# A hybrid mLSTM/Hyena encoder block on one core: two-input elementwise work taken from GpSimd and given to VectorE

## The chip, the cores and the metric

The kernel runs on one core of a Trainium2 chip. The metric is the time of one execution on the device in microseconds (us). TensorE (PE) does the matrix products and transposes, VectorE (DVE) and ScalarE (ACT) the elementwise work, GpSimd (POOL) elementwise work, masks and some DMAs, and SyncE (SP) issues most of the DMAs. Each engine works through its own queue in order, and waits there for what the other engines deliver.

## The reference

One encoder layer on 512 tokens of width 1024, in fp32:

```
h  = rms_norm(x) * (1 + scale1) + shift1            # modulation from c @ w_ada
p  = h @ w_in + b_in                                # q, k, v, o, gates | x1, x2, z of Hyena
y_m = mLSTM(q, k, v, o, gates)                      # 4 heads x 128, forward + backward, chunkwise
z  = x1 * long_conv(z, filter0); z = x2 * long_conv(z, filter1); y_h = rms_norm(z)   # FFT convolution
x  = x + gate1 * (concat(y_m, y_h) @ w_out)
x  = x + gate2 * expert_choice_moe(rms_norm(x) * (1 + scale2) + shift2)   # 16 experts, 64 tokens each, ff 2048
out = rms_norm(x)
```

The weights of the 16 experts are 3 x 8 MB each and are read once.

## The kernel before

**Precision by halves.** In the projections an fp32 operand is split into a high half (fp32r, made by ScalarE's `act.copy` or a VectorE cast) and a low half, `lo = v - hi`. `split` (L240) does this for the weights: high half at L241 on ScalarE, low half at L242 on VectorE or GpSimd. A weight piece has 128 x 1024 elements. The same subtraction stands at L320 for the filter weights, at L499 for the tokens and at L848 for the mixer's result. The mLSTM result passes through `split` too (L804), always on VectorE.

**Front part.** Up to about 460 us the kernel computes filters and their spectra (`spectrum`, L359: sums and differences at L374/L376 from PSUM, combined by `put` at L383), the modulation (`ada`, L429; bias added at L452), the token operand (L491 to L500), the projections (`in_chunk`, L535, with the short convolution in `conv`, L560), the long convolutions (`long_conv`, L601: complex products at L615 to L617, `fold` and its `put` at L621), the heads (`stage`, `weighted`: scaling by the normaliser and sum of both directions at L786 to L795), Hyena's norm (L837), the output projection and the router.

**Order.** The phases are written in the order of `ORDER` (`Z C0 K Q X1 G I0 V C1 H0 H1 X2 I1 H2 O H3`). The Tile framework places the instructions in each engine's queue from a model of their times and from priorities; the output projection and the router are pinned by hand. Every instruction then runs in its queue's order.

**Two-input work on two engines.** The table `SHARE` (L113) has a pattern for each of eleven places, and `ew(site)` (L247) walks through it: a `p` puts the next instruction on GpSimd, a `v` on VectorE. What GpSimd does besides: masks (`affine_select`, L742 and L919), fills, the one-hot copies at L1233, one multiplication of 128 x 1024 per token tile (L984), and DMAs (L415, L450, L1110, L1121, L1145, L1167).

**Experts.** From about 460 us on, expert weights stream through a ring of eight 2 MB buffers (`ring`, L1079, SP's queue). A load into a buffer waits until TensorE has read what was there. The first loads also wait for space that the front part still holds.

Of the kernel before, what the change touches and what calls it, by code (L numbers as in the profile page):

```python
# [108 lines left out]
TEMPS = {"H": 4, "I": 3, "V": 2, "M": 5}  # L109

BANKS = {"P": 3, "S": 2, "R": 3}

SHARE = {"heads": "ppvvpppppvvvvvvv", "spectra": "vvvvvppp", "products": "vvpvpp", "folds": "vvpvvvvpvvppvvpv", "norm": "pppppvpv", "w3": "pvppvvpv", "filters": "p", "tokens": "vvpvvpvv", "w_in": "vp", "w_out": "vvpppppv", "mix": "vvvp"}  # L113

PACE = (1, 0, 2, 1, 1, 2, 1, 1, 1, 0, 2, 2, 2, 2)

# [17 lines left out]
def body(tc, a, out, dbg=None):  # L134
# [4 lines left out]
    with ExitStack() as ctx:  # L139
# [97 lines left out]
            k = i.shape[0]  # L237
            pin(pe.transpose(o, i, ident[0:k, 0:k]))  # L238

        def split(v, hi, lo, eng=None):  # L240
            act.copy(hi, v)  # L241
            (eng or dve).tensor_tensor(lo, v, hi.bitcast(F32), op=OP.subtract)  # L242


        _k = {}

        def ew(site):  # L247
            n = _k[site] = _k.get(site, -1) + 1
            return pool if SHARE[site][n % len(SHARE[site])] == "p" else dve

        def rstd_steps(o, v, ss, scale, eps, tag="rs"):

# [31 lines left out]
        with first(PF):  # L284
            hcol = hyp[:, H_B:H_B + 3]
            hid, sins = None, []
            for l in range(2):
                ps = bank("S")
                for q in range(2):
                    h = slice(64 * q, 64 * q + 64)  # L290
                    if l == 0:
                        mm(ps[h, 0:256], hyp[0:33, H_W1:H_W1 + 64], hyp[0:33, 256 * q:256 * q + 256])
                    else:
                        mm(ps[h, 0:256], hyp[h, H_W2:H_W2 + 64], hid[h, :])
                ar, kk = t2("H", n=256), t2("H", n=256)
                dve.tensor_scalar(ar, ps[:, 0:256], hcol[:, l:l + 1], hcol[:, 2:3], op0=OP.add, op1=OP.mult)
                dve.tensor_scalar(kk, ar, 1.0 / (2 * math.pi), MAGIC, op0=OP.mult, op1=OP.add)
                dve.tensor_scalar(kk, kk, MAGIC, None, op0=OP.subtract)
                c1 = 6.28125
                c2 = float(np.float32(math.floor((2 * math.pi - c1) * 2 ** 23) / 2 ** 23))  # L300
                c3 = 2 * math.pi - c1 - c2
                for c in (c1, c2, c3):
                    dve.scalar_tensor_tensor(ar, kk, -c, ar, op0=OP.mult, op1=OP.add)
                dve.tensor_scalar(ar, ar, 3.1415925, -3.1415925, op0=OP.min, op1=OP.max)
                hid = t2("H", n=256)
                sins.append(act.activation(hid, ar, AF.Sin).ins)


            hidp = t2("H", dt=F32R)
            his = [slice(64 * q, 64 * q + 64) for q in range(2)]  # L310
            for q, lo in enumerate(his[::-1]):
                hi, c = his[q], slice(256 * q, 256 * q + 256)
                dve.tensor_copy(hidp[hi, c], hid[hi, :])
                dve.tensor_tensor(hidp[lo, c], hid[hi, :], hidp[hi, c].bitcast(F32), op=OP.subtract)
            w3h, w3l = slot8("s", F32R), slot8("l", F32R)
            for b in (2, 3, 0, 1):
                bs = slice(b * 512, (b + 1) * 512)
                with tc.issue_after(sins[W3A]):
                    act.copy(w3h[:, bs], w3[:, bs])
                ew("w3").tensor_tensor(w3l[:, bs], w3[:, bs], w3h[:, bs].bitcast(F32), op=OP.subtract)  # L320

        sel4 = slot8("h", F32R)
        dve.tensor_copy(sel4[0:4, 0:512].rearrange("p (b m) -> p b m", b=4),
# [35 lines left out]
        def spectrum(Xc, Xs, uc, us, scale=None):  # L359

            def pair(u, cs, r, ops):

                p0, p2 = bank("S"), bank("S")
                mm(p2, dft(0, r + 2, cs), u[:, r + 2, :])
                mm(p0, dft(0, r, cs), u[:, r, :])
                f2 = t2("H")
                if scale is None:
                    act.copy(f2, p2)
                else:
                    act.mul(f2, p2, scale)  # L370
                o = [t2("H")] if len(ops) > 1 else []
                for v, op in zip(o + [f2], ops):
                    if scale is None:
                        dve.tensor_tensor(v, p0, f2, op=op)  # L374
                    else:
                        dve.scalar_tensor_tensor(v, p0, scale, f2, op0=OP.mult, op1=op)  # L376
                return o + [f2]

            both, add, sub = (OP.add, OP.subtract), (OP.add,), (OP.subtract,)

            def put(X, terms):
                for m, p, q, op in terms:
                    ew("spectra").tensor_tensor(X[:, m], p, q, op=op)  # L383

            ac, bc = pair(uc, 0, 0, both)
            cc, dc = pair(uc, 0, 1, both) if uc is us else pair(uc, 0, 1, add) + pair(us, 0, 1, sub)
            put(Xc, ((0, ac, cc, OP.add), (2, ac, cc, OP.subtract)))
            cs_, ds = pair(us, 1, 1, both) if uc is us else pair(us, 1, 1, add) + pair(uc, 1, 1, sub)
            put(Xc, ((1, bc, ds, OP.subtract), (3, bc, ds, OP.add)))
            as_, bs = pair(us, 1, 0, both)  # L390
            put(Xs, ((0, as_, cs_, OP.add), (2, as_, cs_, OP.subtract),
                     (1, bs, dc, OP.add), (3, bs, dc, OP.subtract)))

        KF = {}
        kfd = dp.tile([2, 128, 2048], F32, name="kfd")
        for o in (1, 0):
            plus, minus = q4(slot8("s")), q4(slot8("s"))
            for q in range(4):
                hs = []
                for d in range(2):  # L400
# [7 lines left out]
                        act.activation(wn, dab[:, bs], AF.Exp, scale=negt[:, q:q + 1])  # L408
                    dve.scalar_tensor_tensor(wn, wn, 0.05, ps, op0=OP.add, op1=OP.mult)
                    hs.append(wn)  # L410
                ew("filters").tensor_tensor(plus[:, q, :], hs[0], hs[1], op=OP.add)  # L411
                ew("filters").tensor_tensor(minus[:, q, :], hs[0], hs[1], op=OP.subtract)
                if q == 0:
                    hb = t2("I", 1, 512)
                    pool.dma_start(hb, a["hy_bias"][0, o:o + 1, :])  # L415
# [57 lines left out]
        with first(2000):  # L473
# [17 lines left out]
            for k in range(8):  # L491
                ps = bank("R")
                for i in range(4):
                    transpose(ps[:, i * 128:(i + 1) * 128], xt[i][:, k * 128:(k + 1) * 128])
                v = t2("I")
                act.activation(v, ps, AF.Identity, bias=mod1[:, 0, k:k + 1], scale=A1[:, k:k + 1])
                hi, lo = (t[k // 4][:, (k % 4) * 512:(k % 4 + 1) * 512] for t in (hh, hl))
                dve.tensor_copy(hi, v)
                ew("tokens").tensor_tensor(lo, v, hi.bitcast(F32), op=OP.subtract)  # L499
                hT.append((hi, lo))  # L500

        scr = dp.tile([2, 1024], F32, name="scr")
# [19 lines left out]
        def prep():  # L522

            if not halves:
                return
            c0, g = halves.pop(0)
            with first(PRIO):
                wh, wl = (slot8(t, F32R).rearrange("p (k c) -> p k c", k=8) for t in "hl")
                for t in (0, 4):
                    w = half2(n=4)  # L530
                    last_in[0] = sp.dma_start(w, w_in[:, t:t + 4, c0 + 256 * g:c0 + 256 * g + 256]).ins
                    split(w, wh[:, t:t + 4], wl[:, t:t + 4], ew("w_in"))
            ready.append((c0, wh, wl))

        def in_chunk(c0, done, tokens=False):  # L535
# [65 lines left out]
        def long_conv(u, o):  # L601
# [6 lines left out]
            for m in range(4):  # L608
# [3 lines left out]
                    act.dma_start(kf[:, m % 2], kfd[:, :, m * 512:(m + 1) * 512].rearrange("a p c -> p a c"))  # L612
                t = [t2("H") for _ in range(3)]
                for o_, p, q in ((t[0], c, kc), (t[1], s, ks), (t[2], c, ks), (s, s, kc)):
                    ew("products").tensor_tensor(o_, p, q, op=OP.mult)  # L615
                ew("products").tensor_tensor(c, t[0], t[1], op=OP.subtract)
                ew("products").tensor_tensor(s, t[2], s, op=OP.add)  # L617

            def put(terms):
                for o_, p, q, op in terms:  # L620
                    ew("folds").tensor_tensor(o_, p, q, op=op)  # L621

            def fold(Y):

# [146 lines left out]
        def weighted(h, d, pt):  # L771
# [11 lines left out]
            dve.reciprocal(nr, nr)  # L783
            nb = nr.unsqueeze(2).to_broadcast([128, 4, 128])
            if d == 0:
                ew("heads").tensor_tensor(hs4[:, :, h, :], pv[:, :, 0:128], nb, op=OP.mult)  # L786
                return
            ew("heads").tensor_tensor(pv[:, :, 0:128], pv[:, :, 0:128], nb, op=OP.mult)
            ew("heads").tensor_tensor(hs4[:, :, h, :], hs4[:, :, h, :], pv[:, :, 0:128], op=OP.add)
            for ti in range(4):  # L790
                junk = small(128, tag="jk", bufs=1)
                act.activation(junk, hs4[:, ti, h, :], AF.Square, accum_out=hss[:, ti, h:h + 1])
            hrs = small(4, tag="hrs")
            rstd(hrs, hss[:, :, h], 128, tag="r4")
            ew("heads").tensor_tensor(hs4[:, :, h, :], hs4[:, :, h, :], hrs.unsqueeze(2).to_broadcast([128, 4, 128]),  # L795
                              op=OP.mult)

        def head_out(h):
# [22 lines left out]
        def gated_2():  # L821
# [12 lines left out]
            zrs = small(16, tag="zrs", bufs=1)  # L834
            rstd(zrs, zss.rearrange("p r g -> p (r g)"), 128, tag="r16")
            for r in range(4):
                ew("norm").tensor_tensor(z2[:, r], z2[:, r], zrs[:, 4 * r:4 * r + 4].unsqueeze(2).to_broadcast([128, 4, 128]),  # L837
                                   op=OP.mult)
            mixh, mixl = slot8("s", F32R), slot8("s", F32R)
            for c in range(4):  # L840
# [4 lines left out]
                v = t2("H")  # L845
                act.activation(v.rearrange("p (i r) -> p r i", r=4), q4(ps), AF.Copy, scale=col(VG_H + c))
                dve.tensor_copy(mixT[4 + c][0], v)
                ew("mix").tensor_tensor(mixT[4 + c][1], v, mixT[4 + c][0].bitcast(F32), op=OP.subtract)  # L848

        def output_gates():  # L850
            def o_done(c, ps):
# [32 lines left out]
        for q, g, t0 in ((0, 1, "h"), (0, 0, "h"), (1, 1, "x"), (1, 0, "y")):  # L884
# [3 lines left out]
            for n in range(2):  # L888
                w = half2()
                sp.dma_start(w, w_out[:, 4 * g + 2 * n:4 * g + 2 * n + 2, q * 512:(q + 1) * 512])  # L890
                split(w, wh[:, 2 * n:2 * n + 2], wl[n], ew("w_out"))
            for k in range(4):
                wo[q, 4 * g + k] = (wh[:, k, :], wl[k // 2][:, k % 2, :])
        xt = load_x("aa")
# [387 lines left out]
```

## Time and profile before

| what | value |
|---|---|
| median of 3 runs | 1411.64 us (1408.95 to 1413.45) |
| profiled execution, its own time | 1409.65 us |
| its span (first to last instruction) | 1407.9 us |
| PE busy | 1292.6 us, 92% of the span |
| DVE busy | 530.3 us, 38%, 959 instructions |
| ACT busy | 255.7 us, 18% |
| POOL busy | 207.3 us, 15%, 174 instructions |
| HBM read | 460.53 MB, 330 GB/s over the span |

The busy shares are averages over a front part in which the elementwise engines work hard and an expert part in which they hardly work. Time in front of the span and behind it is 1409.65 - 1407.9 = 1.75 us. In the rows below, an instruction's duration is the time in the record of it; the next one on the engine often starts some 80 ns before the record ends.

### The profile page before, as it was taken

How to read it: one execution, taken by the hardware profiler on the slowest of the kernel's cores; microseconds unless marked ns; L12 is line 12 of the kernel's file. 1: busy time of each engine (PE TensorE's matmuls, PEld its weight loads, DVE VectorE, ACT ScalarE, POOL GpSimd, SP SyncE). 2: the span in 40 equal slices, each digit the busy share in tenths (PEclk: the TensorE clock that was granted, in tenths of full speed). 3: DMA queues.
4: the chain of work that ended last, by engine and by line, in shares of the span. 5: the costliest groups of instructions: out<-in, count | busy, mean ns of one | idle time of the engine just before them, and what ended most of it. 6: DMA issues, size and time to landing. Idle time of an engine off the chain costs nothing.

```text
span 1407.9 us, 14559 instructions
## 1 busy us (share of the span) xinstructions
PE 1292.6 (92%) x5845; PEld 602.2 (43%) x5845; DVE 530.3 (38%) x959; ACT 255.7 (18%) x557; POOL 207.3 (15%) x174
## 2 busy tenths in 40 slices
PE   6899989989695899999998999998999999899986
PEld 2366557657574333433432432343243343334322
DVE  6776895497837022212212122121122212212131
ACT  5333231336511010110100100001010010101110
POOL 5432671295502000000000000000000000000000
PEclk9999999999897999999999999999999999999999
DMA  9543444352515799999999999999999999999995
GB/s 329 184 172 120 155 140 122 128 187 77 198 61 209 311 399 427 426 428 427 426 427 427 427 426 426 426 426 429 425 427 426 427 427 427 427 426 426 427 410 223
DMA packets 57971, 466.07 MB, mean 331 GB/s; under 512 B 5416, under 2 KB 20008, under 8 KB 32432
## 3 DMA queue, kind: packets, MB, share of 16 engines
q1 hardware_dynamic: 53344, 455.56, 79.2%
q10 hardware_dynamic: 3216, 5.65, 1.3%
q0 software_dynamic: 1344, 3.94, 0.8%
q8 instruction: 46, 0.75, 0.2%
q14 instruction: 21, 0.17, 0.0%
HBM read 460.53 MB, written 4.60 MB: 330 GB/s over the span
## 4 chain that ended last, share of the span: by engine, by line
PE 60%; DMA 19%; DVE 11%; issue 5%; ACT 2%; POOL 2%; POOLq 0%; SPq 0%; ACTq 0%; DVEq 0%
PE ps L178 56%; DMA r<-in_w_up_dram 16%; PE ps L238 3%; DMA out_dram<-a 2%; DVE H L615 1%; DVE l L242 1%; DMA b<-in_hy_w_dram 1%; DMA M<-cmd 1%; DVE M L1228 0%; ACT I L1227 0%; DVE s L621 0%; POOL l L242 0%; DVE M L989 0%; DVE M L991 0%; POOL M L742 0%
## 5 line engine op out<-in xcount | busy, mean ns | idle before, releaser
L178 PE MATMUL ps<-r,x 128*64 128x512 f32 x2048 | 505.8, 611 | 37.8 <-DMA r<-in_w_up_dram 33.6
L178 PEld LDWEIGHTS ps<-r,x 128*64 128x64 f32 x2048 | 143.4, 139 | 306.1 <-issue 245.0
L178 PE MATMUL ps<-r,M 128*64 128x512 f32 x1024 | 231.9, 598 | 7.3 <-DVE M L1228 6.8
L1177 DVE SCALAR_TENSOR_TENSOR a<-ps,aff,a 128x512 f32<-128x512 f32 x120 | 90.1, 751 | 153.4 <-PE ps L178 153.4
L1233 POOL COPY H<-M 128x256 f32<-128x256 f32 x30 | 11.1, 400 | 807.5 <-DVE M L1187 606.6
L178 PEld LDWEIGHTS ps<-r,M 128*64 128x64 f32 x1024 | 69.1, 136 | 130.1 <-issue 117.5
L1217 DVE COPY I<-ps 128x512 f32<-128x512 f32 x32 | 22.1, 692 | 250.8 <-PE ps L178 231.8
L1219 ACT COPY I<-ps 128x512 f32<-128x512 f32 x32 | 18.8, 586 | 496.4 <-PE ps L178 496.4
L178 PE MATMUL ps<-b,h 128*128 128x512 f32 x192 | 83.8, 436 | 0.7 <-DVE b L499 0.6
L178 PE MATMUL ps<-a,h 128*128 128x512 f32 x192 | 81.7, 430 | 2.1 <-DVE x L566 2.1
L178 PE MATMUL ps<-a,l 128*128 128x512 f32 (+1 forms) x200 | 81.9, 410 | 0.0
L1228 DVE TENSOR_TENSOR M<-ps,I 128x256 f32<-128x256 f32 x64 | 27.2, 425 | 144.0 <-ACT I L1227 142.2
L178 PEld LDWEIGHTS ps<-M,h 128*128 128x128 f32 x512 | 63.3, 198 | 24.3 <-issue 18.6
L178 PE MATMUL ps<-M,h 128*128 128x128 f32 x512 | 68.9, 289 | 1.5 <-DVE M L1187 1.5
L178 PEld LDWEIGHTS ps<-V,H 128*128 128x128 f32 x120 | 22.3, 186 | 97.4 <-DVE a L1177 78.7
L178 PE MATMUL ps<-V,H 128*128 128x512 f32 x120 | 60.0, 500 | 0.0
L178 PE MATMUL ps<-s,d 128*128 128x512 f32 x112 | 57.5, 611 | 1.8 <-POOL s L411 1.1
L238 PEld LDWEIGHTS ps<-par,I 128*128 128x128 f32 x268 | 36.2, 208 | 47.9 <-issue 38.9
L1227 ACT ACTIVATE I<-ps 128x256 f32<-128x256 f32 x64 | 24.6, 384 | 167.4 <-PE ps L238 167.4
L238 PE MATMUL ps<-par,I 128*128 128x128 f32 x268 | 46.2, 305 | 7.5 <-DVE I L452 6.7
L242 POOL TENSOR_TENSOR l<-w,h 128x1024 fp32r<-128x1024 f32 x16 | 42.3, 2644 | 66.6 <-ACT h L241 51.1
L1102 DVE TENSOR_SCALAR x<-ps,A,mod 128x128 f32<-128x128 f32 x32 | 13.1, 410 | 99.5 <-PE ps L178 99.5
(329 smaller groups left out, 1369.6 us busy)
## 6 DMA issues: line engine op xcount, KB each, us to landing
r<-in_w_gate_dram SPq DMA_DIRECT2D x64, 2048.0 KB, 27.4
r<-in_w_up_dram SPq DMA_DIRECT2D x64, 2048.0 KB, 31.3
r<-in_w_down_dram SPq DMA_DIRECT2D x63, 2048.0 KB, 24.1
w<-in_w_ada_dram SPq DMA_DIRECT2D x40, 512.0 KB, 4.7
w<-in_w_in_dram SPq DMA_DIRECT2D x28, 512.0 KB, 4.7
w<-in_w_out_dram SPq DMA_DIRECT2D x8, 512.0 KB, 4.0
a<-in_w_ada_dram SPq DMA_DIRECT2D x2, 1024.0 KB, 17.0
b<-in_w_ada_dram SPq DMA_DIRECT2D x2, 1024.0 KB, 15.1
```

The costliest lines, as they stand in the source:

```text
L178: return pin(pe.matmul(o, l, r, start=start, stop=stop))
L238: pin(pe.transpose(o, i, ident[0:k, 0:k]))
L242: (eng or dve).tensor_tensor(lo, v, hi.bitcast(F32), op=OP.subtract)
L615: ew("products").tensor_tensor(o_, p, q, op=OP.mult)
L1102: dve.tensor_scalar(xsT[:, k, :], v, A2[:, k:k + 1], mod2[:, 0, k:k + 1], op0=OP.mult, op1=OP.add)
L1177: dve.scalar_tensor_tensor(xs, ps, aff[:, i, e:e + 1], xs, op0=OP.mult, op1=OP.add)
L1217: dve.tensor_copy(gs, gu[j])
L1219: act.copy(gs, gu[j])
L1227: act.activation(sg, pv[:, :, 0, :], AF.Silu)
L1228: dve.tensor_tensor(hidT[j // 2][:, j % 2 * 4:j % 2 * 4 + 4, :], pv[:, :, 1, :], sg, op=OP.mult)
L1233: pool.tensor_copy(o2[:, :, q, :], oh[:, :, e % 2, :])
```

## The change

`SHARE` and `ew` go, and everything that was handed out by them is written as `dve.tensor_tensor`. `split` loses its engine argument. Nothing else is edited; L984's multiplication, the masks, the fills, the copies at L1233 and GpSimd's DMAs stay where they are.

```diff
-SHARE = {"heads": "ppvvpppppvvvvvvv", "spectra": "vvvvvppp", "products": "vvpvpp", "folds": "vvpvvvvpvvppvvpv", "norm": "pppppvpv", "w3": "pvppvvpv", "filters": "p", "tokens": "vvpvvpvv", "w_in": "vp", "w_out": "vvpppppv", "mix": "vvvp"}
...
-        def split(v, hi, lo, eng=None):
+        def split(v, hi, lo):
             act.copy(hi, v)
-            (eng or dve).tensor_tensor(lo, v, hi.bitcast(F32), op=OP.subtract)
+            dve.tensor_tensor(lo, v, hi.bitcast(F32), op=OP.subtract)
...
-                ew("w3").tensor_tensor(w3l[:, bs], w3[:, bs], w3h[:, bs].bitcast(F32), op=OP.subtract)
+                dve.tensor_tensor(w3l[:, bs], w3[:, bs], w3h[:, bs].bitcast(F32), op=OP.subtract)
...
-                    ew("spectra").tensor_tensor(X[:, m], p, q, op=op)
+                    dve.tensor_tensor(X[:, m], p, q, op=op)
...
-                ew("filters").tensor_tensor(plus[:, q, :], hs[0], hs[1], op=OP.add)
-                ew("filters").tensor_tensor(minus[:, q, :], hs[0], hs[1], op=OP.subtract)
+                dve.tensor_tensor(plus[:, q, :], hs[0], hs[1], op=OP.add)
+                dve.tensor_tensor(minus[:, q, :], hs[0], hs[1], op=OP.subtract)
...
-                ew("tokens").tensor_tensor(lo, v, hi.bitcast(F32), op=OP.subtract)
+                dve.tensor_tensor(lo, v, hi.bitcast(F32), op=OP.subtract)
...
-                    split(w, wh[:, t:t + 4], wl[:, t:t + 4], ew("w_in"))
+                    split(w, wh[:, t:t + 4], wl[:, t:t + 4])
...
-                    ew("products").tensor_tensor(o_, p, q, op=OP.mult)
-                ew("products").tensor_tensor(c, t[0], t[1], op=OP.subtract)
-                ew("products").tensor_tensor(s, t[2], s, op=OP.add)
+                    dve.tensor_tensor(o_, p, q, op=OP.mult)
+                dve.tensor_tensor(c, t[0], t[1], op=OP.subtract)
+                dve.tensor_tensor(s, t[2], s, op=OP.add)
...
-                    ew("folds").tensor_tensor(o_, p, q, op=op)
+                    dve.tensor_tensor(o_, p, q, op=op)
...
-                split(w, wh[:, 2 * n:2 * n + 2], wl[n], ew("w_out"))
+                split(w, wh[:, 2 * n:2 * n + 2], wl[n])
```

The four places of `heads` (L786, L788, L789, L795), `norm` (L837) and `mix` (L848) are edited in the same way.

## Rows read from the trace of the kernel before

**Rows 1.** The page's slices of 35.2 us: busy tenths of three engines.
```profile
PE   6899989989695899999998999998999999899986
...
DVE  6776895497837022212212122121122212212131
...
POOL 5432671295502000000000000000000000000000
```

**Rows 2.** Busy time by stretch: PE, PEld, DVE, ACT, POOL, then clock and DMA.
```profile
60.00:82.00 22.00, 15.52 (x67) 10.24 (x68) 21.69 (x25) 8.80 (x13) 17.19 (x11) 0.92 0.62 214
140.00:202.00 62.00, 54.96 (x226) 36.01 (x224) 56.44 (x55) 17.16 (x23) 45.35 (x35) 0.99 0.43 133
280.00:345.00 65.00, 60.34 (x260) 41.17 (x259) 60.53 (x94) 30.48 (x100) 48.40 (x32) 0.95 0.42 134
358.00:383.00 25.00, 13.70 (x81) 11.78 (x82) 23.67 (x52) 14.46 (x39) 12.45 (x7) 0.77 0.57 212
```

**Rows 3.** Waits of the whole run: total us, times, longest.
```profile
PE ps L238 <- DVE k L795: 8.7, 1, 8.7
```

**Rows 4.** Groups of POOL: count, busy us, mean ns, then idle before and releasers.
```profile
L242 POOL TENSOR_TENSOR l<-w,h 128x1024 fp32r<-128x1024 f32 x16 | 42.3, 2644 | 66.6 <-ACT h L241 51.1 <-PE ps L178 15.4
L617 POOL TENSOR_TENSOR s<-H,s 128x512 f32<-128x512 f32 x8 | 12.6, 1570 | 0.8 <-DVE s L615 0.8
...
L742 POOL TENSOR_SCALAR_AFFINE_SELECT M<-M 128x512 f32<-128x512 f32 x8 | 9.0, 1131 | 15.0 <-DMA M<-cmd 15.0
...
L795 POOL TENSOR_TENSOR k<-k,hrs 128x512 f32<-128x512 f32 x1 | 1.0, 1040 | 5.3 <-DVE hrs L267 5.3
```

**Rows 5.** DVE instructions in order of time, 369 to 380 us: start, duration.
```profile
369.25 0.42 DVE L847 CAST s<-H 128x512 fp32r<-128x512 f32 x1
...
374.47 1.22 DVE L242 TENSOR_TENSOR j<-w,y 128x1024 fp32r<-128x1024 f32 x1
375.60 0.16 DVE L266 TENSOR_TENSOR r<-r,r 128x4 f32<-128x4 f32 x1
...
378.36 0.69 DVE L789 TENSOR_TENSOR k<-k,M 128x512 f32<-128x512 f32 x1
378.96 0.69 DVE L242 TENSOR_TENSOR s<-M,s 128x512 fp32r<-128x512 f32 x1
```

**Rows 6.** One POOL and one DVE instruction in order of time, at 371 us.
```profile
371.03 2.34 POOL L242 TENSOR_TENSOR j<-w,y 128x1024 fp32r<-128x1024 f32 x1
...
371.13 2.27 DVE L260 TENSOR_SCALAR r<-r 128x4 f32<-128x4 f32 x1
```

**Rows 7.** Groups of DVE in the stretch 140 to 202 us.
```profile
L242 DVE TENSOR_TENSOR l<-w,h 128x1024 fp32r<-128x1024 f32 x4 | 10.5, 2622 | 2.5 <-ACT h L241 2.5
L615 DVE TENSOR_TENSOR H<-s,k 128x512 f32<-128x512 f32 x4 | 7.1, 1773 | 0.0
...
L596 DVE SCALAR_TENSOR_TENSOR x<-I,x 128x512 f32<-128x512 f32 x4 | 5.8, 1456 | 1.5 <-ACT I L595 1.5
...
L565 DVE SCALAR_TENSOR_TENSOR x<-ps,vcol,x 128x511 f32<-128x511 f32 x4 | 3.0, 746 | 0.1
...
L564 DVE TENSOR_TENSOR x<-x,ecol 128x2 f32<-128x2 f32 x4 | 2.8, 702 | 0.8 <-ACT x L563 0.8
```

**Rows 8.** Groups of DVE in the stretch 60 to 82 us, the largest.
```profile
L498 DVE CAST a<-I 128x512 fp32r<-128x512 f32 x6 | 5.9, 1002 | 0.2 <-ACT I L496 0.2
```

**Rows 9.** Groups of DVE in the stretch 280 to 345 us, the largest.
```profile
L615 DVE TENSOR_TENSOR H<-s,k 128x512 f32<-128x512 f32 x8 | 9.1, 1152 | 0.0
```

**Rows 10.** Groups of DVE in the stretch 358 to 383 us, the largest.
```profile
L847 DVE CAST s<-H 128x512 fp32r<-128x512 f32 x4 | 4.7, 1183 | 0.8 <-ACT H L846 0.8
```

**Rows 11.** Groups of POOL in the stretch 140 to 202 us, the largest.
```profile
L242 POOL TENSOR_TENSOR l<-w,h 128x1024 fp32r<-128x1024 f32 x4 | 11.5, 2872 | 14.3 <-ACT h L241 14.3
```

**Rows 12.** Busy time in the expert part, columns as in the second group.
```profile
540.00:1380.00 840.00, 800.05 (x3626) 303.17 (x3622) 181.24 (x316) 81.90 (x171) 13.50 (x33) 0.99 1.01 426
```

**Rows 13.** Waits of SP's queue: total us, times, longest.
```profile
SPq L1088 <- PE ps L178: 886.1, 133, 44.0
```

More of the change, by code (lines that the diff above doesn't have):

```diff
@@ L238, in transpose @@
             pin(pe.transpose(o, i, ident[0:k, 0:k]))
-        def split(v, hi, lo, eng=None):
+        def split(v, hi, lo):
             act.copy(hi, v)
-            (eng or dve).tensor_tensor(lo, v, hi.bitcast(F32), op=OP.subtract)
[L245 to L249, printed above, removed]
+            dve.tensor_tensor(lo, v, hi.bitcast(F32), op=OP.subtract)
         def rstd_steps(o, v, ss, scale, eps, tag="rs"):
@@ L785, in weighted @@
             if d == 0:
-                ew("heads").tensor_tensor(hs4[:, :, h, :], pv[:, :, 0:128], nb, op=OP.mult)
+                dve.tensor_tensor(hs4[:, :, h, :], pv[:, :, 0:128], nb, op=OP.mult)
                 return
-            ew("heads").tensor_tensor(pv[:, :, 0:128], pv[:, :, 0:128], nb, op=OP.mult)
-            ew("heads").tensor_tensor(hs4[:, :, h, :], hs4[:, :, h, :], pv[:, :, 0:128], op=OP.add)
+            dve.tensor_tensor(pv[:, :, 0:128], pv[:, :, 0:128], nb, op=OP.mult)
+            dve.tensor_tensor(hs4[:, :, h, :], hs4[:, :, h, :], pv[:, :, 0:128], op=OP.add)
             for ti in range(4):
@@ L794, in weighted @@
             rstd(hrs, hss[:, :, h], 128, tag="r4")
-            ew("heads").tensor_tensor(hs4[:, :, h, :], hs4[:, :, h, :], hrs.unsqueeze(2).to_broadcast([128, 4, 128]),
+            dve.tensor_tensor(hs4[:, :, h, :], hs4[:, :, h, :], hrs.unsqueeze(2).to_broadcast([128, 4, 128]),
                               op=OP.mult)
@@ L836, in gated_2 @@
             for r in range(4):
-                ew("norm").tensor_tensor(z2[:, r], z2[:, r], zrs[:, 4 * r:4 * r + 4].unsqueeze(2).to_broadcast([128, 4, 128]),
+                dve.tensor_tensor(z2[:, r], z2[:, r], zrs[:, 4 * r:4 * r + 4].unsqueeze(2).to_broadcast([128, 4, 128]),
                                    op=OP.mult)
@@ L847, in gated_2 @@
                 dve.tensor_copy(mixT[4 + c][0], v)
-                ew("mix").tensor_tensor(mixT[4 + c][1], v, mixT[4 + c][0].bitcast(F32), op=OP.subtract)
+                dve.tensor_tensor(mixT[4 + c][1], v, mixT[4 + c][0].bitcast(F32), op=OP.subtract)
         def output_gates():
```

## The prediction

> **What bounds the kernel now.** I read the page's slices first. TensorE is busy nearly throughout, VectorE is at six tenths or more in most of the first thirteen slices, and GpSimd works in these alone [rows 1]. From 540 us on the DMA engines are the limit, at 426 GB/s and a share of 1.01, and GpSimd is busy for 13.5 us of 840, with none of the moved instructions [rows 12]. The waits of SP's queue show what starts that part: the loads of expert weights (L1088) wait 886.1 us in 133 waits for TensorE's matmuls [rows 13]. So the expert part begins when TensorE has finished the front, and what the front gains or loses is passed on one for one.
>
> Next I looked for stretches of the front in which TensorE has gaps while VectorE has none. There are four, by the windows [rows 2]: A, 60 to 82 us, DVE busy 21.7 of 22 and PE idle 6.5; B, 140 to 202, DVE 56.4 of 62 and PE idle 7.0; C, 280 to 345, DVE 60.5 of 65 and PE idle 4.7; D, 358 to 383, DVE 23.7 of 25 and PE idle 11.3. The waits name the longest gap, 8.7 us in D, as one for VectorE's normalisation of a head at L795 [rows 3]. The four gaps sum to 29.5 us. The granted clock is 0.92 in A, 0.95 in C and 0.77 in D [rows 2]: TensorE loses some clock by its gaps.
>
> **Is VectorE really that busy?** The reader should see in D a VectorE instruction on four columns that lasts 2.27 us, from 371.13 to 373.40, while a GpSimd instruction runs from 371.03 to 373.37 [rows 6]. Instructions on four columns beside it take 0.16 us [rows 5]. It ends with the GpSimd instruction: it was held by it. In stretch B the same is seen in the means: 2.62 us for a low half of 128x1024 [rows 7] that takes 1.22 with GpSimd at rest [rows 5]; 1.77 and 1.46 us for products of 128x512 [rows 7] that take 0.69 [rows 5]. Instructions that read PSUM (L565, 0.75 us) show nothing of it [rows 7]. GpSimd pays as well: 1.57 us at L617, where the least disturbed of its 128x512 instructions, L795, took 1.04 [rows 4].
>
> **The change, part by part.** It moves 98 instructions, in 22 groups of GpSimd of which the first and the last are shown [rows 4]: 19 of 128x1024 and 79 of 128x512, 168 us of GpSimd time. On VectorE one of 128x1024 starts the next 1.13 us after itself, one of 128x512 after 0.60 us [rows 5]. So 19 x 1.13 + 79 x 0.60 = 69 us are added to VectorE. What goes away is the time in which GpSimd holds VectorE. I count it as, for each group of VectorE instructions without a PSUM source, its count times its mean less the undisturbed duration (1.22, 0.69, 0.16 us, and 0.42 for a cast [rows 5]).
>
> Stretch B in full: L242 4 x (2.62 - 1.22) = 5.6; L615 into H with k 4 x (1.77 - 0.69) = 4.3; L596 4 x (1.46 - 0.69) = 3.1; L564 on x 4 x (0.70 - 0.16) = 2.2 [rows 7]; seven smaller groups of the same view 7.7. Sum 22.9 us. Moved there: four of 128x1024 [rows 11] and 19 of 128x512, 4.5 + 11.4 = 15.9 us. Net -7.0.
>
> The others by the same count. A: held 9.3 us, of which the casts at L498 6 x (1.00 - 0.42) = 3.5 [rows 8]; moved two and eight, 7.1; net -2.2. D: held 8.2 us, of which the casts at L847 4 x (1.18 - 0.42) = 3.1 [rows 10]; moved five and one, 6.3; net -1.9. C: held 22.2 us, of which L615 8 x (1.15 - 0.69) = 3.7 [rows 9]; moved two and 26, 17.9. In C four of the masks of L742 stay on GpSimd, at a mean of 1.13 us [rows 4]. They hold VectorE for 0 us (if each meets an instruction with a PSUM source) to 4.5; I take 4, since VectorE has hardly a pause there, and C's net is -0.3 (-4.3 to +0.2).
>
> Together -11.4 us of VectorE time. What of it reaches the end? In A and D VectorE is saturated and TensorE waits for it, so I count all. In B the first 46 us have no gap of TensorE; the saving there shortens a backlog of VectorE that TensorE meets only at the end of the stretch, and cannot return more than the 7.0 us of gaps. I count 5. Sum -2.2 - 5 - 0.3 - 1.9 = -9.4 us.
>
> Against this stands a new wait. 13 of the moved instructions in the four stretches are low halves of weights, which need ScalarE's high half (L241). GpSimd could stand idle for it; now VectorE waits, and behind it in its queue stand the convolution (L564 to L566), the products and the heads, for which TensorE and ScalarE wait. The price is 0 (the framework puts the subtraction late enough) up to 0.63 us each, as VectorE's own four waited in B [rows 7], which is 8.1. I take half, +4.0, because the row is the worst of the four stretches.
>
> The other 31 moved instructions lie where TensorE has no gaps to speak of: six of 128x1024 and 25 of 128x512, 21.8 us, against 21 us that VectorE is held there. They are hidden by TensorE's matmuls; were that cover gone they would cost about 1 us net, 21.8 at the most. GpSimd's DMAs (L415, L450) and masks (L742) now stand behind fewer instructions and can only start earlier. Their bound is a gain of the length of one GpSimd instruction in front of them, 1 to 2.6 us [rows 4]; I take nothing. Likewise nothing for the clock that TensorE gets back; at most D's 0.23 of 13.7 busy us, 3 us.
>
> **Sum.** -9.4 + 4.0 = -5.4 us, on 1409.65: 1404.2 for an execution like the profiled one. That one lies 2.0 us under the median of the runs, so 1406.2 is the predicted median. Its own range is -14 (no new wait, clock regained) to 0, 1398 to 1412.
>
> **Rivals.** (1) *VectorE inherits GpSimd's waits.* GpSimd's low halves stood idle 66.6 us in all, 51.1 of it for ScalarE, 3.2 us for each of 16 [rows 4], and 14.3 us in B alone [rows 11]. In one queue such a wait stops everything behind it. At 0.63 to 3.2 us for 13 instructions the price is 8 to 42 us; VectorE's own row is the nearer, so I take 1.5 each, 19.5 us: -9.4 + 19.5 = +10, or 1422. It is slower from 1.05 us a piece (13.6 us) on. For it: VectorE is the engine that all wait for in these stretches. Against it: VectorE's row has 0.63, where it was as busy.
>
> (2) *GpSimd was real help.* If the hold were no cost of GpSimd's work (the long VectorE instructions having another cause), 69 us would be added and nothing removed: 7.1 + 15.9 + 17.9 + 6.3 = 47 us in the four stretches, less VectorE's idle 0.3 + 5.6 + 4.5 + 1.3 = 11.7, makes +35, or 1447. The Trainium skill ("Perfetto Trace Analysis", section "Optimizing Scalar/DVE Operations") says that with a saturated VectorE it may pay to offload work to ScalarE or even to GpSimd, which would speak against this change; it adds that these two share a read port into SBUF, so that offloading between them might not help. The four-column instruction of 2.27 us that ends with GpSimd's [rows 6] speaks against the rival.
>
> (3) *TensorE's gaps close.* If VectorE was late only by the backlog that the holds built up, all 29.5 us of gaps go: 1382. Against it: after the change VectorE is still busy for some 60 of 65 us in C and 22 of 25 in D.
>
> (4) *No effect.* A gap is ended by something else that stands just behind VectorE (ScalarE is busy for 14.5 of D's 25 us [rows 2]), or the queue is ordered anew and the gain is lost elsewhere: 1411.6. That the change does nothing because the work isn't moved is excluded by the rows: 98 instructions of GpSimd come from the edited lines.
>
> **How the numbers follow.** A change under 0.3% (4.2 us) can hardly be told from none on this kernel. The forecast's case has 0.46: its middle is 1.2 us beyond that bound, but what I left at nothing (clock, masks and DMAs earlier) all points down, so I give 0.36 of it to faster and 0.10 to the same. Rival 1 has 0.28, rival 2 0.04, rival 3 0.08, rival 4 0.14. Faster 0.36 + 0.08 = 0.44, same 0.10 + 0.14 = 0.24, slower 0.28 + 0.04 = 0.32. The range goes from 1391 (most of rival 3 is left out) to 1425 (rival 2 and the dearer part of rival 1 are left out).
>
> **What the profile after would show.** GpSimd's busy time falls by about 168 us, to some 40. VectorE's busy time of the run changes by under 15 us around 530; 128x1024 low halves take 1.22 us each and L615's products 0.69. L564 returns to 0.16 us. In the four stretches TensorE's idle sum falls from 29.5 towards 24. If rival 1 holds, VectorE's idle time before L242, released by ScalarE, is over 13 us in the front. If rival 2 holds, the means at L615 and L242 stay long. The expert part keeps its 426 GB/s and its length. The prediction is wrong in its working if the long instructions on VectorE stay, if the expert part itself changes, or if the new order of the queues moves gaps to places that had none.

## The result, and the profile after

The changed kernel takes 1385.7 us (median of 4 runs, 1383.09 to 1387.55) beside 1410.3 for the kernel before (1405.48 to 1413.45): ratio 0.9824, 95% interval 0.9807 to 0.984. That is 24.6 us faster, 20.5 us under the forecast and outside its range. The profiled execution took 1383.09 us with a span of 1381.4.

The page of the changed kernel: busy time of the engines, the slices of 34.5 us, and the chain that ended last.
```profile
PE 1280.7 (93%) x5845; PEld 602.6 (44%) x5845; DVE 516.3 (37%) x1057; ACT 255.5 (18%) x557; POOL 40.2 (3%) x76
...
PE   6999999998795999999989999998999899899996
...
DVE  6766795798564121231211212121221222212131
...
POOL 1000000000011000000000000000000000000000
...
PE 74%; DMA 18%; DVE 5%; issue 2%; ACT 1%; POOLq 0%; ACTq 0%; POOL 0%; SPq 0%; DVEq 0%
```
GpSimd's time fell from 207.3 to 40.2 us. VectorE has 98 instructions more, and still 14 us less busy time than before (530.3). The time lay in the front: its end moved from 460.3 to 436.8 us. The expert part got 3 us shorter (947.6 to 944.6), at 426 GB/s as before (540 to 1350 us).

The windows below cut both fronts at equal progress of TensorE, counted in matmuls, so that a row of the one answers to a row of the other (the order of the matmuls is not the same in both). Columns are as in [rows 2]. The kernel before, its whole front last:
```profile
39.20:85.40 46.20, 39.72 (x152) 17.71 (x152) 37.83 (x46) 16.49 (x24) 24.32 (x16) 0.96 0.50 159
85.40:168.30 82.90, 82.90 (x342) 54.84 (x342) 58.52 (x68) 27.05 (x37) 27.89 (x15) 1.00 0.44 145
168.30:211.30 43.00, 35.96 (x160) 25.44 (x159) 39.14 (x43) 12.11 (x16) 31.97 (x28) 0.96 0.48 149
297.90:364.70 66.80, 58.50 (x263) 40.75 (x263) 57.37 (x108) 39.07 (x122) 45.87 (x31) 0.95 0.38 126
364.70:392.90 28.20, 19.43 (x97) 16.75 (x97) 19.82 (x49) 8.30 (x26) 6.81 (x5) 0.76 0.37 142
...
0.00:460.30 460.30, 400.37 (x1797) 263.29 (x1797) 329.57 (x602) 163.33 (x363) 192.72 (x140) 0.95 0.48 162
```
The changed kernel:
```profile
38.00:73.30 35.30, 32.02 (x133) 15.98 (x133) 29.99 (x53) 13.13 (x18) 0.53 (x1) 0.95 0.48 155
73.30:162.70 89.40, 87.61 (x357) 56.36 (x357) 57.13 (x91) 30.52 (x43) 0.00 (x0) 1.00 0.50 165
162.70:195.30 32.60, 32.60 (x161) 25.30 (x160) 30.46 (x53) 12.35 (x17) 4.12 (x12) 1.00 0.45 132
281.50:344.00 62.50, 55.68 (x262) 40.25 (x262) 54.88 (x131) 38.86 (x125) 3.35 (x6) 0.95 0.46 158
344.00:369.50 25.50, 17.26 (x99) 15.03 (x98) 17.20 (x53) 7.99 (x22) 0.00 (x0) 0.80 0.23 83
...
0.00:436.80 436.80, 388.75 (x1797) 260.60 (x1797) 315.62 (x700) 163.28 (x363) 25.63 (x42) 0.96 0.50 170
```
Rows 1 and 2 belong together, since the cut between them differs (152 and 133 matmuls in the first): 129.1 us became 124.7 (A and the stretch behind it, in which TensorE hardly pauses and so covers VectorE's work, -4.4). Row 3 is the core of B: 43.0 became 32.6, -10.4. There TensorE's gaps of 7.0 us are gone, and its busy time is 3.4 us less; of that the granted clock, 1.00 instead of 0.96 over 43 us, makes 1.7. C lost 4.3 and D 2.7 us. These four make -21.8 of the front's -23.5. Over the front half comes from gaps (59.9 to 48.0 us) and half from shorter busy time of TensorE for as many matmuls, 1797 (400.4 to 388.8). These are rows of one execution each. In a second profile of the changed kernel (the run beside the last experiment below, 1389.96 us) the front took 441.6 us; most of the 4.8 us more lie in its first 42 us, and the stretches behind these agree within 0.4 us.

What became of the long instructions is in the groups of VectorE, first a group of the front before, then three of the changed front. L240, L606 and L612 answer to L242, L615 and L621 of before.
```profile
L242 DVE TENSOR_TENSOR l<-w,h 128x1024 fp32r<-128x1024 f32 x16 | 31.8, 1991 | 14.6 <-ACT h L241 9.2 <-PE ps L178 5.3
```
```profile
L240 DVE TENSOR_TENSOR l<-w,h 128x1024 fp32r<-128x1024 f32 x32 | 38.4, 1222 | 19.7 <-ACT h L239 19.4 <-PE ps L176 0.3
...
L612 DVE TENSOR_TENSOR s<-s 128x512 f32<-128x512 f32 x16 | 10.8, 685 | 0.0
...
L606 DVE TENSOR_TENSOR H<-s,k 128x512 f32<-128x512 f32 x16 | 10.6, 687 | 0.0
```
The durations shown are back at their undisturbed values: twice as many low halves (32 for 16) take 38.4 us where 16 took 31.8 (a mean of 1991 ns), and the products of [rows 7, 9] are at 0.69. Counted as in the prediction (each group's count times its mean above the undisturbed value), VectorE was held for 82 us of the front before and for 4.4 after. The idle time before these low halves, waiting for ScalarE, doubled from 9.2 to 19.4 us.

The waits of TensorE that are left in the changed front:
```profile
PE ps L236 <- DVE k L786: 8.2, 1, 8.2
PE ps L236 <- DVE mx L1025: 6.9, 1, 6.9
PE ps L176 <- DVE pt L758: 6.1, 1, 6.1
```
The first is the wait of [rows 3], nearly unchanged: D kept its longest gap. None names L240.

### The profile page after: what moved, and what is told of

The parts are those of the page before. It is cut to its first block, busy times and chain, and to the rows that moved or that the text cites. A ratio compares the mean times of both kernels' runs of the same rounds, so it can differ in the third digit from the quotient of the medians.

```text
span 1381.4 us, 14513 instructions
## 1 busy us (share of the span) xinstructions
PE 1280.7 (93%) x5845; PEld 602.6 (44%) x5845; DVE 516.3 (37%) x1057; ACT 255.5 (18%) x557; POOL 40.2 (3%) x76
## 4 chain that ended last, share of the span: by engine, by line
PE 74%; DMA 18%; DVE 5%; issue 2%; ACT 1%; POOLq 0%; ACTq 0%; POOL 0%; SPq 0%; DVEq 0%
PE ps L176 71%; DMA r<-in_w_up_dram 14%; PE ps L236 4%; DMA out_dram<-a 2%; DMA M<-cmd 1%; DVE M L982 0%; DMA par<-in_par_dram 0%; DVE M L1219 0%; DVE M L980 0%; ACT I L1218 0%; DVE a L1111 0%; DMA w<-in_w_in_dram 0%; DVE s L839 0%; DVE a L898 0%; DVE M L794 0%
## 5 line engine op out<-in xcount | busy, mean ns | idle before, releaser
L176 PEld LDWEIGHTS ps<-r,x 128*64 128x64 f32 x2048 | 146.5, 139 | 300.0 <-issue 244.7
L176 PE MATMUL ps<-b,h 128*128 128x512 f32 x192 | 79.8, 417 | 0.0
L176 PEld LDWEIGHTS ps<-a,h 128*128 128x128 f32 x192 | 36.4, 190 | 23.3 <-issue 9.5
L240 DVE TENSOR_TENSOR l<-w,h 128x1024 fp32r<-128x1024 f32 x32 | 38.4, 1222 | 19.7 <-ACT h L239 19.4
```

Of the source, the lines that this page charges most:

```text
L176: return pin(pe.matmul(o, l, r, start=start, stop=stop))
L240: dve.tensor_tensor(lo, v, hi.bitcast(F32), op=OP.subtract)
```

## Experiments

**Are the holds the cause?** A pair that differs only in what GpSimd does. Both are the changed kernel; after each instruction that was moved (except those of `w_out`), GpSimd also works on data that nobody needs: multiplications of 128x256 that read SBUF in one, fills of 128x64 that only write in the other. The data are a piece of the parameters that gets a tile and a load of its own (`wrt`). TensorE, VectorE and ScalarE have the same instructions in the same order in both runs; it is not quite the changed kernel's order (at 279 of the first 1797 places another matmul stands).

```diff
+                n = int(np.prod(o.shape[1:]))      # o: output of the moved instruction
+                for _ in range(n // 256):          # f1_read
+                    pool.tensor_tensor(wrt, wrt, one.to_broadcast([128, 256]), op=OP.mult)
+                for _ in range(n // 64):           # f2_fill
+                    pool.memset(extra, 0.0)
```


> The changed kernel, plus 214 multiplications of 128x256 on GpSimd (two SBUF inputs, by one) that nothing waits for; all engines but GpSimd have the same order as in f2_fill. Theory H (GpSimd's two-input work holds VectorE, and these holds were what the kernel before lost): VectorE's SBUF-only instructions are long again as far as the extra work reaches (about 12 to 150 us), and it is 8 to 20 us slower than f2_fill. Theory O (the gain came from the new order of the queues): the same as f2_fill within 4 us.

> The changed kernel, plus 856 fills of 128x64 on GpSimd that read nothing and that nothing waits for. Both theories: 1386, within 5 us of the changed kernel; VectorE's L564 at 0.16 us and its 128x1024 subtractions at 1.22 us. If GpSimd's work of any kind holds VectorE, it is as slow as f1_read.

Multiplications: 1419.72 us (ratio 1.0071, interval 1.0048 to 1.0094). Fills: 1396.32 (0.9917, 0.9899 to 0.9935). They are 23.4 us apart, more than the 8 to 20 expected, and the fills are 5 us over the upper end of theirs. The added work kept GpSimd busy for 181 and 133 us. VectorE, in the run with multiplications and then in the one with fills:
```profile
L255 DVE TENSOR_TENSOR l<-w,h 128x1024 fp32r<-128x1024 f32 x16 | 22.0, 1373 | 0.0
...
L633 DVE TENSOR_TENSOR H<-s,k 128x512 f32<-128x512 f32 x12 | 9.8, 828 | 0.0
...
L584 DVE SCALAR_TENSOR_TENSOR V<-ps,vcol,V 128x511 f32<-128x511 f32 x12 | 8.8, 741 | 0.0
```
```profile
L255 DVE TENSOR_TENSOR l<-w,h 128x1024 fp32r<-128x1024 f32 x16 | 19.5, 1217 | 0.0
...
L584 DVE SCALAR_TENSOR_TENSOR V<-ps,vcol,V 128x511 f32<-128x511 f32 x12 | 8.8, 742 | 0.0
L633 DVE TENSOR_TENSOR H<-s,k 128x512 f32<-128x512 f32 x12 | 8.1, 682 | 0.0
```
Two inputs in SBUF are held (1373 for 1217 ns, 828 for 682), an instruction with a PSUM source is not (741, 742). The Trainium skill ("SBUF — State Buffer", section "Who interferes with whom") says the same: VectorE with two SBUF inputs contends with a GpSimd instruction that reads SBUF, and not with one that only writes it. The trace agrees.

The 23.4 us between the two were not yet the price of the holds. In the run with multiplications a bias load (L468) left late, behind GpSimd's own work, and VectorE stood 7.2 us waiting for it. So two more pairs: half the work, with which GpSimd is not behind, and all of it with those loads issued by SyncE.

```diff
-                for _ in range(n // 256):     # f3: half the work; fills n // 128
+                for _ in range(n // 512):
...
-                pool.dma_start(m[32 * j:32 * j + 32, :],     # f4, all the work
+                sp.dma_start(m[32 * j:32 * j + 32, :],
```


> As the run with 214 multiplications of 128x256 on GpSimd, with half of them (107). Same order on TensorE, VectorE, ScalarE and SyncE as its partner with fills. In the full run a bias load (L468) left 7.2 us late for VectorE, because it stood behind the multiplications in GpSimd's queue; with half the work GpSimd should no longer be behind. Theory 'the holds cost': half of the 34 us of holds remain, and at 0.69 us for each the run is 8 to 13 us longer than the partner. Rival 'the queue cost' (the 23.4 us came from loads late behind GpSimd's work): 0 to 3 us.

> The partner: half of the fills (428 of 128x64) in place of the 107 multiplications. Both theories: within 2 us of the run with all 856 fills (1396.3 us, ratio 0.9917), since fills held nothing.

> The run with all 214 multiplications on GpSimd, with the bias loads (L468) issued from SyncE's queue, so that none of them stands behind GpSimd's work. Theory 'the holds cost': it stays 15 to 23 us above its partner. Rival 'the queue cost': less than 8 us above it. The gap of 5.4 us that TensorE had while VectorE worked through held instructions should stay by the first and the two of 3.5 and 1.4 us behind the bias go by both.

> The partner: all 856 fills, bias loads on SyncE's queue. Both theories: 1394 to 1400 us, near the run with the loads on GpSimd's queue, if SyncE's queue does not hold the loads back behind weights.

Half the work: 1403.38 (0.9953, 0.9938 to 0.9969) beside 1396.62 (0.9898, 0.9873 to 0.9923), 6.8 us apart, for 16.4 us more of VectorE's busy time in the front (332.5 for 316.1). That lies between the two expectations, nearer to the holds'. All the work with the loads elsewhere: 1408.81 (0.9995, 0.9978 to 1.0012) beside 1387.34 (0.9836, 0.9811 to 0.9862), 21.5 us apart, as the holds have it, and 1.9 us less than with the loads on GpSimd's queue. The fill run also came down, from 1396.3 to 1387.3, where 1394 to 1400 was expected: it is now at the changed kernel's own time, so 856 fills cost nothing. What the 9 us were is open. It was not late bias loads: in the first fill run no engine waits for one, and with half the fills it was no faster (1396.62). With the loads on SyncE the order changed too (at 175 of the first 1797 matmuls), which no run takes apart.

What a hold does to TensorE is to be seen in the timeline of VectorE in the run with multiplications (loads by SyncE), 194 to 199 us:
```profile
193.91 0.74 DVE L583 SCALAR_TENSOR_TENSOR x<-ps,vcol,x 128x511 f32<-128x511 f32 x1
194.57 0.60 DVE L582 TENSOR_TENSOR V<-V,ecol 128x2 f32<-128x2 f32 x1
195.09 0.68 DVE L633 TENSOR_TENSOR H<-s,j 128x512 f32<-128x512 f32 x1
195.69 1.09 DVE L255 TENSOR_TENSOR H<-s,j 128x512 f32<-128x512 f32 x1
196.71 1.09 DVE L633 TENSOR_TENSOR H<-s,k 128x512 f32<-128x512 f32 x1
197.72 0.74 DVE L584 SCALAR_TENSOR_TENSOR x<-ps,vcol,x 128x511 f32<-128x511 f32 x1
```
and in TensorE's next matmul:
```profile
198.61 0.76 PE L178 MATMUL ps<-a,h 128*128 128x512 f32 x1 [5.38 <-DVE x L584]
```
The convolution at L584 is due for TensorE, and stands behind three instructions of 0.60, 1.09 and 1.09 us that would take 0.16 and 0.69. These three make 1.2 us; the rest of the 5.4 is what VectorE was already behind. In the partner this wait is absent.

Cut at the same matmuls, this pair shows where holds cost: VectorE's 8.7 us more in the first 39 to 45 us go with 5.3 us, 5.7 in A with 2.2, 10.8 in the covered stretch behind it with 2.6, 12.7 in B and behind it with 10.4, and nothing later.

**Does any VectorE time cost as much?** The same multiplications on VectorE itself, 214 of them, nobody waiting for them.

```diff
-                    pool.tensor_tensor(wrt, wrt, one.to_broadcast([128, 256]), op=OP.mult)
+                    dve.tensor_tensor(wrt, wrt, one.to_broadcast([128, 256]), op=OP.mult)
```


> The changed kernel with 214 extra multiplications of 128x256 on VectorE itself (0.34 to 0.42 us each, 73 to 90 us in all; nobody needs their results), GpSimd left alone. The comparison is the run with 856 fills on GpSimd, 1396.3 us, in which VectorE has the same instructions without the extra ones. Theory 'planned work is laid where TensorE covers it': although two to three times the 34 us of holds are added to VectorE, the time rises by at most a third of what the holds cost, 0 to 8 us (1396 to 1404), since the framework knows of these instructions and can put them in pauses of VectorE. Rival 'VectorE's time in the front costs the same whoever causes it' (34 us of holds cost 23.4 us, 0.69 us for each): 73 to 90 us cost 50 to 62 us, 1446 to 1458. Something between, 1410 to 1440, would mean that only part of the planned work finds cover.

1407.65 us (0.9986, 0.9972 to 1.0), 11.3 above the run with fills and GpSimd's bias loads by the medians, 10 by the ratios (they ran on two chips). That partner is the wrong one: it is 9 us slower than the changed kernel for reasons of its own, and there are no fills here. Beside the changed kernel itself on the same chip (run again for the last experiment below, 1387.35) the run is 20.3 us longer. Either way it is over the 8 us of the first theory and far under the 50 to 62 of the rival; beside the changed kernel it is what was expected if only part of the planned work finds cover. In the fronts VectorE's busy time rose by 68 to 69 us (384.2 for 316.1, or for 315.6); in the pair with SyncE's loads the holds raised it by 38.9 us (354.7 for 315.7) for 21.5. That is 0.17 to 0.30 us for each us planned and 0.55 for each us held. One stretch, between the same matmuls (B with what covers it), shows it at equal VectorE time; first the fills (loads by SyncE), then the held run, then the one with planned work:
```profile
165.70:242.50 76.80, 76.80 (x431) 56.95 (x430) 58.98 (x108) 23.93 (x43) 23.67 (x153) 1.00 0.43 136
```
```profile
175.80:263.00 87.20, 80.22 (x430) 58.88 (x429) 71.77 (x109) 23.20 (x42) 40.28 (x46) 0.96 0.38 120
```
```profile
178.60:256.30 77.70, 77.70 (x431) 57.19 (x430) 71.79 (x146) 19.00 (x28) 4.12 (x12) 1.00 0.43 135
```
VectorE is busy for 71.8 us in both of the last two. Held, the stretch is 10.4 us longer, 7.0 in gaps and 3.4 in slower matmuls at a clock of 0.96; planned, 0.9. The framework put 83 of the 214 into the stretch before, where TensorE had cover. Elsewhere planned work was not cheap. These are A, that covered stretch and C in the same run:
```profile
45.80:86.20 40.40, 34.42 (x123) 17.47 (x123) 37.63 (x80) 15.10 (x22) 1.42 (x1) 0.92 0.43 142
86.20:178.60 92.40, 91.04 (x360) 56.52 (x359) 81.79 (x166) 29.47 (x42) 0.00 (x0) 1.00 0.46 155
301.90:370.20 68.30, 58.23 (x257) 40.10 (x256) 64.83 (x174) 41.89 (x141) 9.42 (x8) 0.93 0.41 144
```
Beside the rows of the changed kernel VectorE's time is up by 7.6, 24.7 and 10.0 us, and the stretches are 5.1, 3.0 and 5.8 us longer. So it is B that sets the two prices apart; in A planned work cost more than held (5.1 for 7.6, beside 2.2 for 5.7 in the pair). The order on TensorE and VectorE is another than in the pairs, which the comparison can't take out.

**Which part of the change does it?** Each run writes `v` for some places of the table of the kernel before.

```diff
e3_splits:   "w_in": "v", "w_out": "v"
e4_others:   "v" for all places but "w_in" and "w_out"
p1_filters:  "v" for "w3", "filters", "spectra", "tokens"
p2_products: "v" for "products", "folds"
p3_heads:    "heads": "v", "norm": "v", "mix": "v", "w_out": "v"
```


> Only the low halves of the weights (19 instructions of 128x1024, 50 of the 168 us of GpSimd) go to VectorE; the 79 of 128x512 stay where they were. Theory H: the gain goes with the GpSimd time that is taken away, 30 per cent of 24.6, so -7 us: 1403. Theory O: no relation; anywhere from 1386 to 1415.

> The 79 instructions of 128x512 go to VectorE (118 of the 168 us of GpSimd); the 19 low halves of weights stay where they were. Theory H: 70 per cent of 24.6, -17 us: 1393, and with e3_splits the sum is that of the whole change. Theory O: no relation, the two gains do not add up to 24.6.

> Only the places of the filter and spectrum work and of the tokens (w3, filters, spectra, tokens: 33 of the 98) go to VectorE. Theory H (time comes back where GpSimd's holds are taken away, whatever the rest of the order): most of the lead of the stretch around 60 to 82 us, -8 to -11 us against the kernel before: 1398. Theory O (order by chance): no relation, within 10 us of the kernel before to either side.

> Only the products and folds of the long convolutions (34 of the 98) go to VectorE. Theory H: the lead of the stretches around 140 to 202 and 280 to 345 us, -9 to -14 us: 1397; no lead before 140 us. Theory O: no relation.

> Only the places behind 280 us (heads, norm, mix, and the low halves of w_out) go to VectorE. Theory H: -1 to -4 us, since the changed kernel gained little behind 345 us: 1405. Theory O: no relation.

| moved | time, us | ratio (interval) | held, us (82 before) |
|---|---|---|---|
| weights' low halves | 1413.23 | 1.0038 (1.0021 to 1.0056) | 54 |
| all but these | 1391.08 | 0.9885 (0.9861 to 0.9909) | 29 |
| filters, spectra, tokens | 1394.68 | 0.9887 (0.9857 to 0.9916) | 61 |
| products, folds | 1411.4 | 1.001 (0.9997 to 1.0023) | 56 |
| heads, norm, mix, w_out | 1411.5 | 1.0008 (0.9997 to 1.002) | 70 |

The gain was expected to go with the GpSimd time taken away. Two runs came within 4 us of that (`e4_others`, `p1_filters`), three missed it by 6 to 14 us. The parts don't add up either. The first two are complements: with the medians of the kernel before beside them they make +5.3 and -16.9, together -11.6, where the whole has -24.6. And less hold alone foretells nothing: products and folds took 26 us of it away for no gain, filters and spectra 21 us for -15.0. Each partial move is also ordered anew. The run with the low halves has a gap that the kernel before hasn't, among TensorE's waits:
```profile
PE ps L178 <- DVE x L566: 9.8, 1, 9.8
```
The holds that are left there in B (18 us between 140 and 200, counted as above) now meet a convolution that TensorE needs. I read this as: where a hold falls decides its price, and that changes with each order. No run moves a hold alone, and why the products alone return nothing these runs do not settle. So the pairs show that such holds cost time; how the 24.6 us divide between holds that went and the new order stays open.

**What is left of GpSimd.** One two-input multiplication per token tile (L975) made a scaled copy on ScalarE; and on top of it the row loads of the decay masks (`cm_row`) taken from ScalarE's queue to GpSimd's, now nearly empty.

```diff
-            pool.tensor_tensor(xn2[i], xt[i], rs.to_broadcast([128, 1024]), op=OP.mult)
+            act.activation(xn2[i], xt[i], AF.Copy, scale=rs)
...
-            act.dma_start(c0, cmd[...].to_broadcast([128, 512]))     # i2_pool only
+            pool.dma_start(c0, cmd[...].to_broadcast([128, 512]))
```


> The changed kernel with the last two-input instruction of GpSimd, the multiplication of 128x1024 at L975 (four times), made by ScalarE as a scaled copy; the order of the other engines stays. Theory H: the holds in the stretch of the chained selection go, -2 to -5 us against the changed kernel: 1382. Theory O: 1386, no change.

> The changed kernel unaltered, beside the two that follow: 1383 to 1388 us as before, ratio 0.981 to 0.984.

> The changed kernel with the last two-input multiplication of GpSimd (L975) made a scaled copy on ScalarE. It measured 1383.74 us on another chip beside 1385.7. If the 2.0 us shorter stretch of the selection is real, it comes out 1.5 to 2.5 us under the changed kernel beside it; if it was a difference between the chips, within 1 us.

> The kernel before this one, with the row loads of the decay masks (cm_row) issued from GpSimd's queue, which stands empty after the change, in place of ScalarE's. It aims at TensorE's gap of 6.07 us at 330 us, whose chain goes back to such a load. If the load is late because it is issued late behind ScalarE's work, it comes earlier and 2 to 6 us go (1378 to 1382); if it waits for its buffer, nothing changes (within 1 us of the run before); if another order of the queues comes out, it may also lose some us.

On one chip: the changed kernel 1387.35 (0.9848, 0.9831 to 0.9866), the scaled copy 1384.38 (0.9824, 0.9805 to 0.9843; 1383.74 and 0.9803 on another chip), with the loads moved 1379.35 (0.9785, 0.9762 to 0.9807). The copy's 2 to 3 us are small against the intervals, but the end of the front (from 369.5 us on in the changed kernel), where L975 stands, is 2.0 us shorter in both runs. The loads bring 5.0 us more; the intervals touch, but the slowest of the five runs (1381.77) is under the fastest without the edit (1382.0). Before, the chain of the changed kernel from 325 to 335 us read:
```profile
325.74 5.35 DMA M<-cmd
331.12 3.29 DMA M<-cmd
```
One load was issued by ScalarE at 325.74, the next at 331.12, after ScalarE had waited for the first; GpSimd's masks waited 116.6 us in all for such loads. With the loads in GpSimd's queue that is 19.3 us, ScalarE's own waits for such loads fell from 11.8 to 5.2, and C and D read:
```profile
286.60:348.00 61.40, 55.60 (x265) 39.79 (x265) 58.38 (x143) 40.90 (x127) 4.35 (x8) 0.97 0.46 156
348.00:365.40 17.40, 16.21 (x96) 13.37 (x96) 14.58 (x42) 6.71 (x21) 0.00 (x0) 1.00 0.34 121
```
D takes 17.4 us where it took 25.5, at a clock of 1.00 instead of 0.80. D's long gap, which the waits put down to VectorE's normalisation, went with the late loads; the order on TensorE changed too (at 231 of the first 1797 matmuls), and the kernel before was not run with this edit. This version beats both kernels.

## Why the prediction was wrong

**What bounds the kernel** held: the expert part kept its rate and its length to 3 us, and what the front gained was passed on.

**The hold** held in kind: the long instructions went back to 1.22, 0.69 and 0.16 us, GpSimd's time fell by 167 us (168 foretold), VectorE's total by 14 (under 15 foretold).

**The step that failed** is the netting of held time against moved work. It charged 47 us of moved instructions, and 4 for masks, us for us to the four stretches where GpSimd had run them, against 62.6 us of holds; it left -11.4, of which -9.4 was to reach the end. In the rows of A to D VectorE's busy time fell by 7.8, 8.7, 2.5 and 2.6 us, 21.6 in all (A's row holds 19 matmuls fewer after), and with A's cover the time fell by 21.8. The moved work did not all stay there: GpSimd's instructions in these four rows fell by 61, VectorE's rose by 44; the covered stretch behind A took 23 more (91 for 68) where GpSimd lost 15. What a us costs differs as well: planned VectorE time 0.17 to 0.30 us each, held time 0.55, with the difference made in B. With these the whole would be an estimated 12 to 21 us for the 69 moved against (82 - 4) x 0.55 = 43, or -31 to -22, around the -24.6 measured. The prices come from other holds in another order, and the partial moves warn against more use of them.

Of the 16.4 us between -5.4 and the -21.8 of these rows the new wait makes 4.0, B 5.4, C 4.0, A with its cover 2.2 and D 0.8.

**The cap on B** (5 of the 7.0 us of gaps) was wrong too: it brought 10.4, the whole 7.0 and 3.4 of shorter busy time of TensorE. That term was missing everywhere: 11.6 us over the front, beside a clock set at nothing with a bound of 3. By the granted clock of the rows shown the clock gave back about 3.7 us (1.7 in B, 1.7 in D); what the rest is these rows do not show. C brought 4.3 for 0.3; its four masks, taken at 4 us, hold VectorE for 0.9 in all (at 334.6, for one, a 128x16 instruction takes 0.63 us for its usual 0.17 beside a mask of 0.63).

**The new wait** (+4.0) did not come, and with it rival 1 falls, although its sign appeared: 19.4 us of idle VectorE before L240, over the 13 it named. 17.3 of them lie in the covered stretches 73 to 163 and 195 to 282 us, where none of TensorE's waits names it; B's core has 1.9. An idle sum over the front was a bad sign for it; TensorE's waits would have been the right one. Rival 2 is excluded: GpSimd work that reads SBUF, added at a fixed order, made the long instructions return and the time longer by 21.5 us. The Trainium skill's advice there ("Perfetto Trace Analysis", section "Optimizing Scalar/DVE Operations"), that offloading to GpSimd may pay when VectorE is saturated, did not hold for this work; its caution that offloading between the two might not help did.

**Rival 3** is nearest by its number, 1382, and that is mostly luck. Its reason, that the gaps close, came true in B alone: in the rows shown TensorE's idle time went from 7.0 to 0 there, but only from 6.5 to 5.1 us in A with its cover, 8.3 to 6.8 in C and 8.8 to 8.2 in D, together from 30.6 to 20.1 (29.5 to 24 foretold, for narrower windows). The other half of the gain is shorter busy time. D's gap went only when the row loads left ScalarE's queue. The argument against rival 3, VectorE's busy share after the change, was drawn from the same netting.

## What to carry to other kernels

Do not net work that is moved onto a busy engine us for us against stalls that go. Work that the framework knows can be laid under cover (24.7 us of it cost 3.0 here), and where it is not, it costs (5.1 us for 7.6 in A). A stall lands in front of whatever is due: 12.7 us of stalls cost 10.4 in B, 10.8 us under cover only 2.6. Look at the fastest instance of each instruction on the engine; if the same shape takes twice as long beside another engine's work, the offload is charged there as well as done. And before an idle or a gap is put down to the engine named last, follow its chain back to the transfer that was issued late.

## What the runs showed of the hardware

Fills on GpSimd did not slow VectorE: 856 of 128x64, 133 us, with VectorE's 128x1024 at 1217 ns. 214 multiplications of 128x256 held it so that its busy time rose by 38.9 us, and an instruction on two columns (L582) took 0.57 to 0.60 us for 0.16. GpSimd takes 845 ns for a 128x256 multiplication with two SBUF inputs beside a busy VectorE, which does it itself in 418.

A gap can cost TensorE more than its length. In the first run with multiplications the same 5.4 us without a matmul end at 206.3 us; the 128x512 matmuls, 0.40 us before it, took 0.63 us for the next 6 us and then 0.40 again. In B of the pair with SyncE's loads, where the matmuls come in the same order, gaps of 7.0 us cost 10.4 in all, at a granted clock of 0.96 over the held stretch and 1.00 in its partner.
